# Spacing the steps of four scan cores among the projections of a fused two-block kernel

## The chip, the cores and the metric

The kernel runs on one core of one Trainium2 chip. The metric is the device time of one execution in microseconds (us), the median over runs, so lower is better. Five engines work side by side: TensorE (PE in the profile, its weight loads as PEld), VectorE (DVE), ScalarE (ACT), GpSimd (POOL) and SyncE (SP), which issues the DMAs.

## The reference

Two transformer blocks follow one another on 512 tokens of width 1024, in float32. The first is a two-layer block of mixed attention, and it is not touched here. The second has two layers and works on 768 tokens, 512 latent and 256 context ones. Its first layer mixes tokens by two chunked recurrences run in both directions: an HGRN2 scan and a stabilised mLSTM scan, with four heads each. The outputs are normed per head, gated and projected. What concerns this change is the HGRN2 scan, for one chunk:

```
b = cumsum(logf); b_mid = b[CHUNK//2 - 1]; b_last = b[-1]
A = mask(einsum(q*exp(b - b_mid), k*exp(b_mid - b)))
o = A @ v + (q*exp(b)) @ S
S_new = S*exp(b_last) + (k*exp(b_last - b)).T @ v
```

The mLSTM scan needs, per head and direction, a running sum of log forget gates, a running maximum and exponentials of their differences. That is the gate chain below. Its queries and keys come from a three-tap convolution and a silu.

## The kernel before

Everything here happens in `mixer_ab`, the first layer's mixer of the second block, from about 1209 us to 1661 us of the span. Activations stand with the 1024 features on the partitions in 8 blocks of 128 and the 768 tokens along the free axis, each value split into a high and a low part (`hh`, `hl`). A **projection** (`proj2`, `mm2`, line 1019) multiplies one 128-column unit of weights with all tokens. It loops over the 8 feature blocks and issues six matmuls for each: three passes (high by high, high by low, low by high) on each of two token segments. After each feature block `mm2` calls `tick()`, so a projection has eight **turns**.

What is not a projection hangs on those turns. `later(generator, delay)` puts a generator at the end of a list, and each `tick()` advances the first of the list by one step, after its delay in ticks has run out. The order of PE's instructions is fixed by this program order. For DVE, ACT, POOL and SP the framework picks the order when the kernel is built, by program order as the priority, among what its own timing model takes to be ready. Each engine then runs its list in that order and waits for what an instruction needs. PSUM has 8 banks (tag `b`), SBUF work tiles come from 34 slots (`T()`), and raw weights have 3 buffers (`raw`). Weights come in by SP, are rounded by ACT (`whi`, line 306), and their rest (`wlo`, line 307) is made by POOL in this stage.

The order of the stage, with the turns counted from the first one of the second HGRN projection (the very first is done earlier):

- `hgrn_in(h)` (lines 1209 to 1267) for h = 0, 1, 2 issues four projections of head h: two forget gates, queries and values. Behind the second one stands the **preparation** of the head: sigmoids and a log on ACT, and on DVE a scan (L1234), small factor tiles `fa` (L1243 to L1249, 4 buffers, two to a head) and the scaling of keys (L1257). Head 0 ends at turn 24, head 1 at turn 56, head 2 at turn 88. In `hgrn_in(1)` and `hgrn_in(2)` a step of the gate chain is issued behind each of the first three projections, so behind turns 32, 40, 48, 64, 72 and 80.
- `hgrn_core(h)` (lines 1269 to 1368) has 18 steps. Step 1 transposes the values (L1053, copies on ACT L1059). Steps 2 and 3 make the masked scores of the two directions (L1284, L1286) and scale keys (L1289). Steps 4 and 5, one for each direction, make the **small products** of 32 by 32 (L1301), whose copies go out on DVE (L1303), and scale keys on DVE (L1305) and queries on POOL (L1306). Steps 7 and 8 make blocks of 64 (L1316, ACT copy L1318, scalings L1323). Steps 10 and 11 transpose the keys. Steps 12 to 17 are the recurrence over six 128-token blocks: L1343, L1348 and L1350 on PE, state updates L1355 and L1357 on DVE. Step 18 closes with a norm (POOL L1499, DVE L1501 and L1505). Steps 6 and 9 issue nothing. Core 0 waits 24 turns and takes turns 49 to 66, core 1 takes 67 to 84, core 2 89 to 106.
- The **gate chain** (`gate_chain`, lines 1102 to 1175) has six steps. On DVE: step 1 L1105, L1106 and L1109; step 2 L1114 and two scans of L1123; step 3 L1129 and two scans of L1123; step 4 L1136 to L1146; step 5 L1150 and L1155; step 6 two of L1161. Step 4 stores `cm` by SP (L1147) and step 5 stores `wi` (L1153). A last call queues `by_token`, six and six transposes that the mLSTM heads need.
- Four convolutions `conv(j)` (lines 1181 to 1202, turns 89 to 120): a projection each, then L1191, L1195, L1196, L1197 on DVE and silu on ACT.
- `hgrn_in(3)` (turns 121 to 152). Core 3 follows with a delay of 2 (turns 155 to 172).
- Four value projections (`values`, to turn 184), each followed by `later(mlstm_head(h), 2)`, and eight gate projections (`gate`, to turn 248). The mLSTM heads take turns 175 to 226, and `finish(0)` to `finish(3)` (transposes L1512, DVE L1514) turns 227 to 238.
- After turn 248, `drain()` issues whatever is left in the list with no projection in between. Then come `finish(4)` to `finish(7)`, and `place(h)` for all heads (ACT L339, DVE L340), which writes the operand of the next projection (`out2`, L1607). That one takes features 0 to 6 first and 7 last.

The few lines that fix the order of the stage, and the inner loop of a small-product step:

```
for h in range(3):
    self.later(hgrn_core(h, *hgrn_in(h)), 24 if h == 0 else 0)
for _ in chain:
    pass
for j in range(4):
    conv(j)
self.later(hgrn_core(3, *hgrn_in(3)), 2)
```

```
for i in range(2):
    ko, qo = 64 * i + 32 * d, 64 * i + 32 * (1 - d)
    for t in range(n):
        nc.tensor.matmul(pv[ko:ko + 32, t, qo:qo + 32], ...)
    nc.vector.tensor_copy(am[d][ko:ko + 32, a:a + n, qo:qo + 32], pv[ko:ko + 32, 0:n, qo:qo + 32])
```

Of the kernel before, what the change touches and what calls it, by code (L numbers as in the profile page):

```python
# [259 lines left out]
class Body:  # L260
# [763 lines left out]
    def T(self, dt=F32):  # L1024
        return self.ar.tile([P, self.width], dt, tag="t", bufs=self.nslots, name=self.nm("t"))
# [35 lines left out]
    def mixer_ab(self, r):  # L1061
# [114 lines left out]
        chain = gate_chain()  # L1176
# [4 lines left out]
        def conv(j):  # L1181

            ps = self.proj2(self.SEG, "bqk", j)
            z = T()
            b = self.small(2)
            nc.vector.tensor_copy(b, ps[:, 0, SC:SC + 2])
            nc.vector.memset(z[:, 0:1], 0.0)
            nc.vector.memset(z[:, SC + 1:SC + 2], 0.0)
            nc.vector.memset(z[:, T2 + 2:T2 + 3], 0.0)
            for o, w, bk, s in ((1, SC, 0, 1), (SC + 2, S, 1, 0)):  # L1190
                nc.vector.tensor_tensor(z[:, o:o + w], ps[:, bk, 0:w], r[:, o - 1 - bk:o - 1 - bk + w], ALU.mult)  # L1191
                nc.scalar.activation(z[:, o:o + w], z[:, o:o + w], AF.Identity, bias=b[:, s:s + 1])
            cv = T()
            n = T2 + 1
            nc.vector.tensor_scalar(cv[:, :n], z[:, 1:n + 1], c2("conv", 4 + j), None, ALU.mult)  # L1195
            nc.vector.scalar_tensor_tensor(cv[:, :n], z[:, 0:n], c2("conv", j), cv[:, :n], ALU.mult, ALU.add)  # L1196
            nc.vector.scalar_tensor_tensor(cv[:, :n], z[:, 2:n + 2], c2("conv", 8 + j), cv[:, :n], ALU.mult, ALU.add)  # L1197
            o = T()
            self.act(o[:, 0:SC], cv[:, 0:SC], AF.Silu)
            self.act(o[:, SC:T2], cv[:, SC + 1:n], AF.Silu)  # L1200
            qk.append(o)
# [7 lines left out]
        def hgrn_in(h):  # L1209
            z, zb = [], []  # L1210
            for d in range(2):
                t = T()
                zb.append(self.scaled(t, self.proj2(self.SEG, ("hg", h), d), r))
                z.append(t)
                if h:
                    next(chain, None)
            sg, sn = [], []
            for d in range(2):
                nb = self.small(2)
                nc.vector.tensor_scalar(nb, zb[d], -1.0, None, ALU.mult)  # L1220
                x, y = z[d], T()
                self.both(lambda c, s: self.act(y[:, c], z[d][:, c], AF.Sigmoid, bias=nb[:, s:s + 1], scale=-1.0))
                self.both(lambda c, s: self.act(x[:, c], z[d][:, c], AF.Sigmoid, bias=zb[d][:, s:s + 1]))
                sg.append(x)
                sn.append(y)
            self.log_exp()
            res = []
            for d in range(2):
                f = sg[d][:, :T2]
                nc.vector.tensor_scalar(f, f, omlb[:, d, h:h + 1], lbd[:, d, h:h + 1], ALU.mult, ALU.add)  # L1230
                nc.scalar.activation(f, f, AF.Ln)
                bb = T()[:, :T2]
                sd = (1, -1)[d]
                nc.vector.tensor_tensor_scan(bb[:, ::sd], m32, f[:, ::sd], 0.0, ALU.mult, ALU.add)  # L1234
                mid, last = ((15, 31), (16, 0))[d]
                fi, se = (0, 1)[::(1, -1)[d]]
                b3, b4 = ch(bb, 32), bb.rearrange("p (m i n) -> p m i n", i=2, n=32)

                fa = self.ar.tile([P, 66], F32, tag="fa", bufs=4, name=self.nm("fa"))
                lm = self.ar.tile([P, 12, 2], F32, tag="lm", bufs=2, name=self.nm("lm"))  # L1240
                f1, gk, hv, dec = fa[:, 0:12], fa[:, 12:24], fa[:, 48:60], fa[:, 60:66]
                qh = fa[:, 24:48].rearrange("p (m i) -> p m i", i=2)
                nc.vector.tensor_tensor(lm, b4[:, :, :, last], b4[:, :, :, mid], ALU.subtract)  # L1243
                nc.vector.tensor_tensor(f1, lm[:, :, fi], b4[:, :, se, mid], ALU.add)
                nc.vector.tensor_copy(gk, lm[:, :, se])
                nc.vector.tensor_copy(qh[:, :, fi], b4[:, :, fi, mid])
                nc.vector.tensor_tensor(qh[:, :, se], b4[:, :, se, mid], b4[:, :, fi, last], ALU.add)
                nc.vector.tensor_tensor(hv, b4[:, :, 0, last], b4[:, :, 1, last], ALU.add)
                nc.vector.tensor_tensor(dec, hv[:, ::2], hv[:, 1::2], ALU.add)  # L1249
                nc.scalar.activation(fa, fa, AF.Exp)  # L1250
                bm = f
                nc.vector.tensor_tensor(ch(bm, 32), b3, b3[:, :, mid:mid + 1].to_broadcast([P, 24, 32]), ALU.subtract)
                e1 = bb
                nc.scalar.activation(e1, bm, AF.Exp)
                nc.scalar.activation(bm, bm, AF.Exp, scale=-1.0)
                kk = sn[d][:, :T2]
                nc.vector.scalar_tensor_tensor(kk, kk, omlb[:, d, h:h + 1], bm, ALU.mult, ALU.mult)  # L1257
                res.append([e1, kk, None, fa])
            q = T()
            self.addb(q, self.scaled(q, self.proj2(self.SEG, ("hg", h), 2), r))  # L1260
            if h:
                next(chain, None)
            for d in range(2):
                nc.gpsimd.tensor_tensor(res[d][0], res[d][0], q[:, :T2], ALU.mult)
            vf = T()
            self.addb(vf, self.scaled(vf, self.proj2(self.SEG, ("hg", h), 3), r))
            return vf, res

        def hgrn_core(h, vf, res):
# [4 lines left out]
            for d in range(2):  # L1274
                q, k, _, fa = res[d]
# [15 lines left out]
            for d in range(2):  # L1291
                q, k, _, fa = res[d]

                for a, n in ((0, 2), (2, 4)):
                    ps = self.aux()
                    pv = ps.rearrange("p (t e) -> p t e", e=P)
# [3 lines that stand above are left out]
                            o = (a + t) * P  # L1300
                            nc.tensor.matmul(pv[ko:ko + 32, t, qo:qo + 32], k[:, o + ko:o + ko + 32], q[:, o + qo:o + qo + 32],  # L1301
                                             start=(t == 0), stop=(t == n - 1), skip_group_check=True)
                        nc.vector.tensor_copy(am[d][ko:ko + 32, a:a + n, qo:qo + 32], pv[ko:ko + 32, 0:n, qo:qo + 32])  # L1303
                kh, qb = k.rearrange("p (m n) -> p m n", n=64), ch(q, 32)
                nc.vector.tensor_tensor(kh, kh, fa[:, 12:24].unsqueeze(2).to_broadcast([P, 12, 64]), ALU.mult)  # L1305
                nc.gpsimd.tensor_tensor(qb, qb, fa[:, 24:48].unsqueeze(2).to_broadcast([P, 24, 32]), ALU.mult)  # L1306
                yield
            yield
            for d in range(2):
                q, k, _, fa = res[d]  # L1310

                ko, qo = 64 * d, 64 * (1 - d)
# [22 lines left out]
            for i in range(6):  # L1335
                for d in range(2):
                    q, _, kt, fa = res[d]
# [179 lines left out]
        def place(h):  # L1517

            for a, n in ((0, 2), (2, 4)):
                hc = (slice(CO, CO + SC), slice(LT, LT + S))[a // 2]  # L1520
                self.split(self.hh[:, h, hc], self.hl[:, h, hc], gates[h][0][:, a * P:(a + n) * P])

        for h in range(3):
            self.later(hgrn_core(h, *hgrn_in(h)), 24 if h == 0 else 0)
        for _ in chain:
            pass
        for j in range(4):
            conv(j)
        self.later(hgrn_core(3, *hgrn_in(3)), 2)
        for h in range(4):  # L1530
            values(h)
            self.later(mlstm_head(h), 2)
# [501 lines left out]
```

## Time and profile before

| what | us |
|---|---|
| median of 3 runs (2975.01 to 2976.49) | 2975.02 |
| the profiled execution | 2982.45 |
| its span, first to last instruction | 2980.2 |
| `mixer_ab` in the span, first to last projection | 1208.7 to 1661 |

PE is busy for 95% of the span, DVE for 63%, ACT for 40% and POOL for 19%. The DMA engines carry 93 GB/s on average. The page has the span in 40 slices of 74.5 us. A digit is a busy share in tenths, and the line PEclk is the clock that TensorE was granted. An entry in the list of waits reads as "engine, tile and line that waited <- what released it: us in total, times, the longest". In a timeline a row is start, duration, engine, line and operation, with "[idle before <-releaser]" where the engine stood still ahead of it. Durations on POOL are rough, and ends of matmuls are modelled, so starts are the safer number.

### The profile page before, as it was taken

To read this page: it belongs to the slowest core of one execution; us is meant where nothing else is said; L and a number is where in the kernel's file an instruction comes from. 1 tells how busy PE (TensorE), PEld (TensorE's weight loads), DVE (VectorE), ACT (ScalarE), POOL (GpSimd) and SP (SyncE) were. 2 spreads that over 40 slices of the span, in tenths; PEclk is the share of its full clock that TensorE was granted. 3 is DMA by queue.
4 is the path that set the end of the run, shared out by engine and by line. 5 is a ranking of instruction groups with operands and counts; after the bars stand their busy time and mean duration, and the time that the engine had idled before them with its cause. 6 is when DMAs were issued, how large, how long until landed. Compare 5 with 4: busy or idle time off the path is not lost. (4 is left out here: it accounts for less than half of the span.)

```text
span 2980.2 us, 42310 instructions
## 1 busy us (share of the span) xinstructions
PE 2845.4 (95%) x16554; PEld 2479.1 (83%) x16554; DVE 1874.6 (63%) x3532; ACT 1192.8 (40%) x2085; POOL 560.6 (19%) x437
## 2 busy tenths in 40 slices
PE   9999999999999999978999999999999899999997
PEld 7777888877778888867777988888888888899997
DVE  7679995477689985766544373343335788544445
ACT  5663222346542223523444453122113577532223
POOL 3630000036310001533332140000001420300002
PEclk9999999999999999989999999999999999999998
DMA  4235663331156652210121302221121210233332
GB/s 144 74 99 177 199 195 105 92 111 60 64 184 200 195 166 92 82 34 29 43 88 40 107 29 71 64 64 59 62 64 57 86 43 13 91 96 94 98 92 71
DMA packets 98935, 278.46 MB, mean 93 GB/s; under 512 B 11504, under 2 KB 16880, under 8 KB 98224
## 3 DMA queue, kind: packets, MB, share of 16 engines
q1 hardware_dynamic: 98736, 275.76, 29.4%
q8 instruction: 130, 2.13, 0.3%
q14 instruction: 69, 0.57, 0.1%
HBM read 264.84 MB, written 6.68 MB: 91 GB/s over the span
## 5 line engine op out<-in xcount | busy, mean ns | idle before, releaser
L306 ACT ACTIVATE whi<-raw 128x1024 fp32r<-128x1024 f32 (+1 forms) x363 | 377.9, 1042 | 1218.9 <-PE b L1019 451.3
L1019 PE MATMUL b<-hh,whi 128*128 128x512 f32 (+1 forms) x2000 | 649.3, 325 | 0.0
L1019 PE MATMUL b<-hh,wlo 128*128 128x258 f32 x2000 | 476.2, 320 | 0.0
L1019 PE MATMUL b<-hl,whi 128*128 128x512 f32 (+1 forms) x2000 | 470.5, 317 | 0.0
L307 DVE TENSOR_TENSOR wlo<-raw,whi 128x1024 fp32r<-128x1024 f32 (+1 forms) x321 | 391.7, 1220 | 102.4 <-ACT whi L306 100.6
L1019 PEld LDWEIGHTS b<-hh,whi 128*128 128x128 f32 x2000 | 379.9, 190 | 33.5 <-issue 4.0
L1019 PEld LDWEIGHTS b<-hl,whi 128*128 128x128 f32 x2000 | 349.4, 189 | 50.5 <-issue 0.2
L1019 PEld LDWEIGHTS b<-hh,wlo 128*128 128x128 f32 x2000 | 314.5, 191 | 0.0
L334 PE MATMUL b<-hbl,whi 128*128 128x512 f32 x704 | 275.2, 391 | 2.6 <-DVE hbl L345 2.6
L869 DVE SCALAR_TENSOR_TENSOR junk<-araw,cond 128x512 f32<-128x512 f32 x384 | 271.8, 708 | 8.5 <-ACT cond L355 2.3
L333 PE MATMUL b<-hbh,whi 128*128 128x512 f32 x704 | 275.8, 392 | 1.0 <-ACT hbh L344 1.0
L335 PE MATMUL b<-hbh,wlo 128*128 128x512 f32 x704 | 275.1, 391 | 0.3 <-DVE wlo L307 0.3
L1592 POOL TENSOR_TENSOR acc<-acc,t 128x256 f32<-128x256 f32 (+1 forms) x54 | 48.9, 906 | 1015.0 <-ACT t L1587 1014.1
L1019 PE MATMUL b<-t,whi 128*128 128x512 f32 (+1 forms) x864 | 212.5, 354 | 0.0
L392 POOL TENSOR_TENSOR acc<-acc,sq 128x512 f32<-128x512 f32 (+1 forms) x33 | 47.4, 1437 | 761.9 <-ACT sq L389 761.3
L1019 PEld LDWEIGHTS b<-t,whi 128*128 128x128 f32 x864 | 162.3, 188 | 29.7
L334 PEld LDWEIGHTS b<-hbl,whi 128*128 128x128 f32 x704 | 132.8, 189 | 31.4 <-DVE hbl L345 3.3
L333 PEld LDWEIGHTS b<-hbh,whi 128*128 128x128 f32 x704 | 132.7, 189 | 29.2 <-ACT hbh L344 1.5
L335 PEld LDWEIGHTS b<-hbh,wlo 128*128 128x128 f32 x704 | 132.8, 189 | 28.8 <-DVE wlo L307 1.0
L307 POOL TENSOR_TENSOR wlo<-raw,whi 128x1024 fp32r<-128x1024 f32 x42 | 107.4, 2559 | 188.3 <-ACT whi L306 182.8
L335 PE MATMUL b<-hidh,wlo 128*128 128x512 f32 (+1 forms) x352 | 134.2, 381 | 1.2 <-DVE wlo L307 1.1
L333 PE MATMUL b<-hidh,whi 128*128 128x512 f32 (+1 forms) x352 | 133.8, 380 | 0.0
(452 smaller groups left out, 5754.0 us busy)
## 6 DMA issues: line engine op xcount, KB each, us to landing
raw<-w SPq DMA_DIRECT2D x365, 512.0 KB, 3.5
araw<-ada SPq DMA_DIRECT2D x192, 256.0 KB, 3.0
raw<-w SPq DMA_DIRECT2D x18, 256.0 KB, 2.7
xr<-xd SPq DMA_DIRECT2D x2, 2048.0 KB, 8.2
t<-dm SPq DMA_DIRECT2D x8, 384.0 KB, 5.2
x<-xT SPq DMA_DIRECT2D x8, 256.0 KB, 5.3
kTh<-krh SPq DMA_DIRECT2D x32, 64.0 KB, 2.0
kTl<-krl SPq DMA_DIRECT2D x32, 64.0 KB, 2.0
```

Source lines behind the costliest of these rows:

```text
L306: self.last = nc.scalar.activation(hi[:, :m], r, AF.Copy).ins
L307: self.lo_eng.tensor_tensor(lo[:, :m], r, hi[:, :m].bitcast(F32), ALU.subtract)
L333: t.matmul(out, ah, bh, start=start, stop=False, skip_group_check=True)
L334: t.matmul(out, ah, bl, start=False, stop=False, skip_group_check=True)
L335: t.matmul(out, al, bh, start=False, stop=stop, skip_group_check=True)
L392: nc.gpsimd.tensor_tensor(acc[:, c], acc[:, c], t[:, c], ALU.add)
L869: nc.vector.scalar_tensor_tensor(junk, raw, 1.0, self.cond[:, s, k], ALU.mult, ALU.mult, accum_out=self.adah[:, i, t, s:s + 1])
L1019: t.matmul(ps[:, b, :w_], w[:, s], x[:, o:o + w_], start=(k == 0 and b not in seen), stop=(k == n - 1 and i == 2), skip_group_check=True)
L1592: nc.gpsimd.tensor_tensor(ac, ac, t, ALU.add)
```

## The change

Three edits, all in `mixer_ab`. The generators of the HGRN cores are wrapped so that after each step one turn passes in which nothing of the list is issued. The small products of a bank are issued for both quadrants before the copies. The calls of the gate chain move: one stays in `hgrn_in(1)`, behind the query projection and the preparation, and the others stand before and after the convolutions.

```
@@ in hgrn_in(h)
                 z.append(t)
-                if h:
-                    next(chain, None)
...
             self.addb(q, self.scaled(q, self.proj2(self.SEG, ("hg", h), 2), r))
-            if h:
+            if h == 1:
                 next(chain, None)
@@ in hgrn_core
                             nc.tensor.matmul(pv[ko:ko + 32, t, qo:qo + 32], k[:, o + ko:o + ko + 32], q[:, o + qo:o + qo + 32],
                                              start=(t == 0), stop=(t == n - 1), skip_group_check=True)
+                    for i in range(2):
+                        ko, qo = 64 * i + 32 * d, 64 * i + 32 * (1 - d)
                         nc.vector.tensor_copy(am[d][ko:ko + 32, a:a + n, qo:qo + 32], pv[ko:ko + 32, 0:n, qo:qo + 32])
@@ at the end of mixer_ab
+        def spaced(gen):
+
+            for _ in gen:
+                yield
+                yield
+
         for h in range(3):
-            self.later(hgrn_core(h, *hgrn_in(h)), 24 if h == 0 else 0)
+            self.later(spaced(hgrn_core(h, *hgrn_in(h))), 24 if h == 0 else 0)
+        for j in range(4):
+            next(chain, None)
+            conv(j)
+            next(chain, None)
         for _ in chain:
             pass
-        for j in range(4):
-            conv(j)
-        self.later(hgrn_core(3, *hgrn_in(3)), 2)
+        self.later(spaced(hgrn_core(3, *hgrn_in(3))), 2)
```

## Rows read from the trace of the kernel before

**Rows 1.** The page, parts 1 and 2: busy time of the engines, PE by slice.
```profile
PE 2845.4 (95%) x16554; PEld 2479.1 (83%) x16554; DVE 1874.6 (63%) x3532; ACT 1192.8 (40%) x2085; POOL 560.6 (19%) x437
...
PE   9999999999999999978999999999999899999997
```

**Rows 2.** Busy time by stretch: the four HGRN cores, first transposes to last recurrence step.
```profile
core 0: us, PE busy (x) PEld busy (x) DVE busy (x) ACT busy (x) POOL busy (x), PEclk, DMA share, GB/s
1261.20:1313.16 51.96, 37.31 (x276) 32.79 (x274) 34.37 (x70) 13.52 (x23) 16.83 (x9) 0.80 0.09 25
1315.35:1364.56 49.21, 37.66 (x275) 32.64 (x274) 35.05 (x64) 20.95 (x35) 16.71 (x9) 0.93 0.12 37
1371.86:1411.58 39.72, 35.39 (x274) 31.09 (x275) 21.01 (x46) 11.06 (x19) 10.42 (x7) 0.96 0.10 27
1469.75:1507.56 37.81, 34.91 (x274) 30.83 (x275) 17.79 (x36) 9.16 (x16) 11.43 (x9) 0.95 0.19 57
```

**Rows 3.** Waits of PE from 1205 to 1664 us, the longest six.
```profile
PE b L1301 <- DVE t L1303: 15.8, 16, 5.0
PE b L1301 <- DVE fa L1244: 6.6, 1, 6.6
PE b L1348 <- ACT t L1059: 5.7, 2, 4.3
PE b L1053 <- ACT t L1045: 4.7, 4, 3.3
PE b L1455 <- issue: 3.6, 1, 3.6
PE b L1350 <- DVE hR L1357: 3.3, 2, 1.8
```

**Rows 4.** Timeline of PE, 1653 to 1656 us: the first matmul of two turns.
```profile
1653.06 0.40 PE L1019 MATMUL b<-hh,whi 128*128 128x512 f32 x1
...
1654.12 0.40 PE L1019 MATMUL b<-hh,whi 128*128 128x512 f32 x1
```

**Rows 5.** Waits of PE from 1466 to 1508 us, core 3.
```profile
PE b L1301 <- DVE t L1303: 2.5, 4, 1.3
```

**Rows 6.** Busy time in the 14 us in which core 0 stood still longest (columns as above).
```profile
1261.00:1275.00 14.00, 7.24 (x55) 6.40 (x53) 13.94 (x26) 4.84 (x9) 5.01 (x2) 0.90 0.13 37
```

**Rows 7.** Groups of DVE instructions from 1205 to 1664 us: busy us in all, mean ns.
```profile
L1123 DVE TENSOR_TENSOR_SCAN t<-t,t 32x768 f32<-32x768 f32 x4 | 9.2, 2301 | 0.0
...
L1195 DVE TENSOR_SCALAR t<-t,vec 128x769 f32<-128x769 f32 x4 | 7.9, 1977 | 3.4 <-ACT t L1192 3.4
...
L1514 DVE SCALAR_TENSOR_TENSOR t<-b,vec,t 128x256 f32<-128x256 f32 (+1 forms) x11 | 6.5, 603 | 6.2 <-PE b L1512 6.1
...
L1196 DVE SCALAR_TENSOR_TENSOR t<-t,vec,t 128x769 f32<-128x769 f32 x4 | 4.1, 1022 | 0.1
...
L1191 DVE TENSOR_TENSOR t<-b,acc 128x256 f32<-128x256 f32 (+1 forms) x8 | 4.1, 549 | 0.0
...
L1150 DVE TENSOR_TENSOR t<-so,t 64x768 f32<-64x768 f32 x1 | 2.6, 2605 | 0.0
...
L1155 DVE TENSOR_TENSOR t<-t,t 64x768 f32<-64x768 f32 x1 | 0.9, 942 | 0.0
```

**Rows 8.** Timeline of DVE, 1660 to 1671 us, at the end of the stage.
```profile
1660.49 0.42 DVE L1033 TENSOR_TENSOR t<-b,acc 128x256 f32<-128x256 f32 x1 [2.16 <-PE b L1019]
...
1664.15 2.85 DVE L1514 SCALAR_TENSOR_TENSOR t<-b,vec,t 128x512 f32<-128x512 f32 x5
1666.91 3.83 DVE L340 TENSOR_TENSOR hl<-t,hh 128x256 fp32r<-128x256 f32 x8
```

**Rows 9.** Waits of SP's queue from 1205 to 1664 us: the second store of the chain.
```profile
SPq L1153 <- ACT t L1152: 19.9, 1, 19.9
```

**Rows 10.** Timelines of POOL and of DVE around 1264 us.
```profile
1261.96 3.85 POOL L307 TENSOR_TENSOR wlo<-raw,whi 128x1024 fp32r<-128x1024 f32 x1 [6.85 <-ACT whi L306]
...
1264.53 2.10 DVE L1129 TENSOR_TENSOR t<-t,t 64x768 f32<-64x768 f32 x1
```

## The prediction

> **What bounds the kernel now.** I read the page first. PE is busy for 95% of the span and its slices are full nearly everywhere, with a dent at slices 18 and 19 (1267 to 1416 us), which lie in this stage [rows 1]. So a gain must come from time in which PE stands still or runs at its lower clock, and the stage holds some. Next I cut the stage into the four stretches of the HGRN cores [rows 2]. Each holds the same 16 turns and the same small matmuls, so the four lengths should agree. They are 51.96, 49.21, 39.72 and 37.81 us. The list of PE's waits says what it stood for: 15.8 us for the copies of the small products, 6.6 for the factors `fa`, 5.7 for transposed keys or values, 4.7 for the values of a head, 3.3 for state updates [rows 3]. Where core 0 stood longest, DVE was busy for 13.94 of 14 us [rows 6]. It had the preparation of head 1, two steps of the gate chain and core 0 at once. Over the whole span DVE has room (63%). Its work is only bunched.
>
> **What an undisturbed core would take.** A turn takes 1.06 us [rows 4], so 16 turns take 17.0. The best core took 37.81. Of the 20.8 left, 2.5 are waits for the copies [rows 5]. The granted clock was 0.95 there, which is full speed (2.4 GHz) with a piece at 1.2 GHz, and costs about 0.05 x 37.8 = 1.9. So the small matmuls take about 16.4, and an undisturbed stretch 33.4. The four cores lose 18.6, 15.8, 6.3 and 4.4, together 45.1 us. Before cores 2 and 3 PE also waited for the values of the head, which is most of the 4.7 of [rows 3] (longest 3.3). I take 4.0, so 49 us are within reach.
>
> **Edit 1, the spacing.** Counted out by the program, core 0 now takes turns 49 to 83, core 1 84 to 118, core 2 119 to 153, `by_token` 154, core 3 158 to 192, the mLSTM heads 195 to 246, and `finish(0)` 247 and 248. The projections end at turn 248 as before. No instruction is added. Between two steps there are now two turns, 2.1 us instead of 1.06, in which a copy, a scaling or a state update can land. The cores meet other company:
> - Core 0 meets the end of head 1's preparation, without the chain steps that stood in [rows 6]. Its recurrence (turns 71 to 81) falls beside head 2's preparation, as core 1's does now. That company now costs 4.3 (longest wait for transposed keys) and 3.3 [rows 3]. With twice the gap I take half, 4.
> - Core 1 runs wholly beside the convolutions and the chain. I price this under edit 3.
> - Core 2's recurrence (turns 141 to 151) falls beside head 3's preparation, without chain or convolutions: 3.
> - Core 3 starts 3 turns (3.2 us) later than now, about as long as PE waited for its values (3.3), and then has little beside it: 1.
>
> Core 0's `fa` is in use until turn 79, while head 2 asks for one at turn 72, and there are four. So head 2's factors come later. Core 2 wants them at turn 123, 44 turns on, and that covers it. Tiles live longer. I count at most 30 of the 34 slots in use, so no wait there. If that cover were gone, a projection's evacuation would wait for a core's tile, a turn or two each time.
>
> **Edit 1, the end.** Of four `finish` only the first has a projection over it. Numbers 1 to 3 (18 transposes, 6 DVE instructions) fall into the drain, and `place(0)` to `place(3)` are pushed behind them. Now the last gate is ready at 1660.49 and the last `place` ends at 1670.74, after 10.2 us [rows 8], with DVE as the limit. Afterwards DVE has 14 instead of 8 of L1514 at 0.60 us [rows 7] and 16 instead of 8 of L340 at 3.83/8 = 0.48 [rows 8], which is 3.6 + 3.8 = 7.4 us more, plus one operation of the last norm over 768 elements, 0.9 as for L1155 [rows 7]. The 18 transposes are issued after turn 248 rather than before, so the gates end sooner, by 18 x 0.09 = 1.7 us (a stretch has 274 matmuls [rows 2], 96 of them the turns', and the other 178 take 16.4). Net cost 6.6 us. The next projection takes features 0 to 6 first, but its matmuls come faster (under 1 us a feature) than DVE delivers, so PE waits for nearly all of it. Bounds: 3, if half of the places still fit beforehand, and 12, if the norm of the last mLSTM head lands late and PE restarts at 1.2 GHz.
>
> **Edit 2, copies last.** PE no longer waits inside a bank. That removes 2.5 per undisturbed core [rows 5] and the 8 that head 0 takes of the 15.8 (15.8 less three times 2.6) [rows 3]. All of it is inside the 49. The copies, then the scalings behind them, come no later than now. If DVE is late, the wait goes to the next step that reads the scaled keys, four turns on.
>
> **Edit 3, the chain.** Nothing is added here either. Step 1 stays near head 1, steps 2 to 6 go around convolutions 0 and 1. On DVE they need 9.2 for four scans, 2.6 for L1150 [rows 7], 2.1 for L1129 [rows 10], and L1114, L1146, L1155 and two of L1161 at the 0.94 of L1155, so 4.7. Eight tiny ones in step 4 make about 1 (my estimate). Sum 19.6. A convolution needs 1.98 + 2 x 1.02 + 2 x 0.55 = 5.1 [rows 7]. The stretch of turns 89 to 120 takes 48 us on PE: 32 x 1.06 = 34 and about 14 of core 1's 16.4, as its first three steps are over. DVE has in it the chain 19.6, three convolutions 15.3 (the fourth falls behind), core 1 about 15 (17.79 in core 3's stretch, with two evacuations [rows 2]), and a norm with one evacuation, 3.5. That is 53 us into 48. DVE falls about 5 us behind there, and I take 8 for core 1 with some clock lost. Waits behind this: the chain's two stores now stand in SP's queue among these weight loads. The second held SP for 19.9 us before [rows 9] and delayed no projection, as raw weights are three deep. A projection with four spaced steps takes about 12 us, so two of them cover it. If DVE's lag added over 10 us to that wait, each further microsecond would be PE's. Silu and exponentials alternate once more on ACT, at a 40% load, hidden.
>
> **The Trainium skill against edit 3.** A subtraction on POOL took 3.85 us while DVE was in L1129, and L1129 took 2.10 [rows 10], where L1155, of the same size, took 0.94 and L1150 took 2.6 [rows 7]. The chain's seven two-input operations thus cost between 0.94 and 2.6 each. "SBUF — State Buffer", section "Who interferes with whom", says that a DVE instruction with two SBUF inputs contends with a GpSimd instruction that reads SBUF, and that whoever comes first blocks the other. The trace agrees in the durations just given. By that rule, the chain moved beside core 1's POOL scalings would pay the blocked price throughout, which is the second rival below. The sum above goes by the durations measured.
>
> **Sum.** 49 - (4 + 8 + 3 + 1) - 6.6 = 26.4 us off the profiled execution of 2982.45, so 2956.05. That execution stands 7.43 above the median of the runs shown, and I carry this over: 2948.6. The 3.6 us wait of an mLSTM head [rows 3] and the slow matmuls behind it belong to steps that are not spaced. I leave them, with +-8 for the new company.
>
> **Rivals.**
> 1. *Forecast.* 2948.6, own range 2930 to 2962. Chance 0.66.
> 2. *DVE becomes the bound in the convolutions.* For: 53 into 48 us, and [rows 6] shows what a full DVE does. The chain's seven two-input operations at 2.6 each make 18.2 instead of the 9.4 in my sum (4.7 + 2.6 + 2.1), 8.8 more. With the lag in each of three convolutions core 1 loses 22 instead of 8. Against: each step has twice the gap. 2948.6 + 14 = 2962.6. Chance 0.17.
> 3. *Slower: DVE serves preparations, convolutions and chain ahead of the cores' small updates.* Program order is the priority, and a step's copy is issued behind the whole preparation or convolution that went before. Recurrences of cores 0 and 2 would lose the 8.6 that core 1 loses now plus as much again in clock (17 each), and core 1 some 7 us at each of three boundaries, 21: together 55, more than the 49 recovered. With 6.6 at the end the time is 2975 + 13 = 2988. It decides once a spaced step waits about 1 us on average (42 us over 42 steps that issue DVE work). Against: core 2 beside two convolutions lost 6.3 in all. Chance 0.08.
> 4. *The spacing doesn't do what it says.* What PE gains in the cores is given back where the mLSTM heads are pushed against the gates and the drain: 2975. For: they end 20 turns later. Against: they get as many turns as before and the drain issues only 18 transposes. Chance 0.09.
>
> **Numbers.** What a measurement of this kernel can tell from no change is about 0.2%, 6 us. Case 1 lies below 2969 wholly, case 2 for nine tenths (0.15 of its 0.17); its rest and case 4 are the same. Faster 0.81, same 0.11, slower 0.08. The range: residual waits of 5 and an end of 3 give 2975 - 41 = 2934, and the mLSTM wait could take 4 more off. Residual waits of 30 and an end of 12 give 2975 - 7 = 2968. So 2930 to 2970, which takes in case 2 and leaves out cases 3 and 4.
>
> **What would show it.** Right: the four stretches of 32 turns between first transposes and last recurrence step come to 51 to 59 us each (2 x 17.0 + 16.4 = 50.4 undisturbed, plus my residues), with a granted clock near 1; waits of L1301 for L1303 vanish; the last `place` ends about 17 us after the last gate; DVE is at nine tenths during the convolutions. Wrong: DVE full for over 50 us with PE waiting for L1357 or L1059 there; a long wait of L1019 for weights behind a store; or a stretch from last gate to next projection's seventh feature well over 20 us.

## The result, and the profile after

The changed kernel takes 2940.1 us (median of four runs, 2938.5 to 2943.9) against 2975.8 us for the kernel before (four runs beside it, 2975.0 to 2977.4). The ratio is 0.988, with an interval of 0.9868 to 0.9892: faster by 1.2%, and 8.5 us below the forecast of 2948.6. The profiled execution took 2943.85 us with a span of 2941.8.

The page of the changed kernel, parts 1 and 2, the answer to [rows 1]:

```profile
PE 2824.8 (96%) x16554; PEld 2463.4 (84%) x16554; DVE 1864.7 (63%) x3532; ACT 1197.9 (41%) x2090; POOL 562.6 (19%) x437
...
PE   8999999999999999999999989999999999999997
```

The dent at slices 18 and 19 is gone and the counts of PE and DVE instructions are the same. The next view is the busy time by stretch of the four cores, first transposes to last recurrence step, columns as in [rows 2]:

```profile
1260.04:1320.16 60.12, 52.82 (x372) 46.44 (x370) 43.76 (x92) 26.45 (x42) 24.40 (x11) 0.94 0.13 36
1323.42:1377.73 54.31, 50.98 (x371) 45.27 (x370) 47.50 (x79) 23.48 (x35) 23.87 (x15) 0.97 0.18 54
1380.99:1434.75 53.76, 49.98 (x371) 44.19 (x370) 32.75 (x74) 24.50 (x40) 21.23 (x11) 1.00 0.14 40
1443.59:1492.71 49.12, 49.12 (x371) 43.88 (x370) 19.02 (x41) 12.62 (x21) 14.91 (x11) 1.00 0.23 73
```

Each stretch now holds 32 turns instead of 16, hence some 371 matmuls instead of 275, so the lengths aren't to be set against those before as they stand. Core 3 is the yardstick: PE is busy for all of its 49.12 us at a clock of 1.00. Take 32 turns at 1.06 off, and the small matmuls of a core take 15.2 us by this; with 1.066 for a turn (the five from 1208.85 us on, which hold nothing else, take 5.33) it is 15.0. The waits of PE in this stage, the answer to [rows 3]:

```profile
PE b L1299 <- DVE fa L1247: 3.8, 1, 3.8
PE b L1512 <- DVE t L1505: 3.7, 1, 3.7
PE b L1343 <- DVE t L1191: 3.0, 1, 3.0
PE b L1455 <- issue: 2.6, 2, 2.0
PE b L1348 <- ACT t L1059: 2.6, 1, 2.6
PE b L1350 <- DVE hR L1357: 2.0, 2, 1.5
```

The waits of the small products for their copies, 15.8 us before, are not in this list any more (L1299 is the product's new line, L1301 was its old one). What is left on top is one wait of 3.8 us of core 0's small products, one of 3.0 in core 1, and a new one of 3.7 us at the end, at L1512, which transposes the normed outputs of a head.

Two of the names in this list need care. DVE's instructions count up one semaphore, and the list names the one that ended last before PE went on, which need not be the one that PE needed. The small products read keys and queries and no factor tile. The 3.8 us end when L1287 has scaled the keys of core 0; PE and DVE there:

```profile
1273.63 0.69 PE L1299 MATMUL b<-t,t 128*32 128x32 f32 x24 [3.78 <-DVE fa L1247]
```

```profile
1272.94 0.54 DVE L1287 TENSOR_TENSOR t<-t,fa 128x384 f32<-128x384 f32 x1
1273.40 0.15 DVE L1247 TENSOR_TENSOR fa<-fa 128x6 f32<-128x6 f32 x1
```

The tile that L1247 writes belongs to head 1. The 6.6 us that [rows 3] puts down to L1244 is the same wait: there too the scaling of the keys (L1289) ends 0.15 us before PE starts. So the prediction named the wrong tile for it; that DVE was late with head 1's preparation in front is right. L1343 reads nothing of L1191 either. L1191 empties the bank of a convolution, so this wait is, as I read it, for a free PSUM bank.

**Where the time came from.** The stage, from its first projection to the first matmul of the next stage's projection, took 454.3 us before (1208.8 to 1663.1) and takes 423.5 (1207.6 to 1631.1): 30.9 less. The two as one row each, before and after:

```profile
1208.75:1663.06 454.31, 412.97 (x2602) 348.28 (x2601) 261.76 (x541) 192.24 (x358) 158.14 (x91) 0.95 0.16 49
```

```profile
1207.60:1631.06 423.46, 401.00 (x2602) 340.08 (x2601) 253.13 (x541) 200.28 (x367) 159.54 (x91) 0.98 0.18 54
```

PE stands still for 41.3 us before and 22.5 after (length less busy time), 18.9 less. The same 2602 matmuls keep it busy for 12.0 us less, at a granted clock of 0.98 instead of 0.95. So almost two fifths of the gain is clock.

The spans differ by 38.4. Of the rest 1.2 lies ahead of the stage and 6.4 behind it, in code that the change doesn't touch. The largest piece there, 3.9, is a stretch of later projections; 20 us of it in each kernel, before and then after, from the same instruction on:

```profile
2330.00:2350.00 20.00, 16.06 (x102) 15.16 (x102) 15.83 (x24) 8.61 (x21) 11.01 (x13) 0.84 0.29 106
```

```profile
2297.00:2317.00 20.00, 17.22 (x124) 16.23 (x122) 16.51 (x27) 10.12 (x23) 9.98 (x12) 0.96 0.34 117
```

The same work ran at a granted clock of 0.84 in one and 0.96 in the other. Over the twelve runs below, all of which leave it untouched, the part behind the stage took 1310.6 to 1319.1 us. So up to 8 us between two executions are not the stage's own, and I read parts of the stage from traces and totals from medians. The changed kernel's two profiled executions agree in this part (1310.7 each); whether the stage's end has an effect on it is not shown.

### The profile page after: what moved, and what is told of

Read it like the earlier page. It is cut to its first block, busy times and chain, and to the rows that moved or that the text cites. A ratio compares the mean times of both kernels' runs of the same rounds, so it can differ in the third digit from the quotient of the medians.

```text
span 2941.8 us, 42299 instructions
## 1 busy us (share of the span) xinstructions
PE 2824.8 (96%) x16554; PEld 2463.4 (84%) x16554; DVE 1864.7 (63%) x3532; ACT 1197.9 (41%) x2090; POOL 562.6 (19%) x437
## 5 line engine op out<-in xcount | busy, mean ns | idle before, releaser
L307 DVE TENSOR_TENSOR wlo<-raw,whi 128x1024 fp32r<-128x1024 f32 (+1 forms) x321 | 391.4, 1220 | 97.9 <-ACT whi L306 96.2
L333 PEld LDWEIGHTS b<-hbh,whi 128*128 128x128 f32 x704 | 132.7, 189 | 29.4 <-ACT hbh L344 1.5
L307 POOL TENSOR_TENSOR wlo<-raw,whi 128x1024 fp32r<-128x1024 f32 x42 | 106.3, 2532 | 171.4 <-ACT whi L306 140.3
L1663 DVE COPY sml<-b 128x2 f32<-128x2 f32 x44 | 7.0, 160 | 200.8 <-PE b L1019 200.8
```

What stands on the lines that cost most here:

```text
L307: self.lo_eng.tensor_tensor(lo[:, :m], r, hi[:, :m].bitcast(F32), ALU.subtract)
L333: t.matmul(out, ah, bh, start=start, stop=False, skip_group_check=True)
L1663: nc.vector.tensor_copy(bu, pu[:, 0, bcol])
```

## The experiments

Twelve runs, five rounds each, against the kernel before beside them (2975.8 to 2976.9 us). The changed kernel, run again at the end:

> The changed kernel itself once more, as the measure on this chip for the other three: 2938 to 2942.

It took 2940.5 us, ratio 0.9881 (0.9867 to 0.9894).

### Which edit brings how much

**Without the spacing** (edits 2 and 3 stay):

```diff
-            self.later(spaced(hgrn_core(h, *hgrn_in(h))), 24 if h == 0 else 0)
+            self.later(hgrn_core(h, *hgrn_in(h)), 24 if h == 0 else 0)
...
-        self.later(spaced(hgrn_core(3, *hgrn_in(3))), 2)
+        self.later(hgrn_core(3, *hgrn_in(3)), 2)
```

> The changed kernel with edit 1 undone: cores step at every turn again, copies stay last, the chain stays around the convolutions. Theory (the time came mostly from the spacing): waits of PE for state updates, transposed keys and scaled keys come back in the cores, while the end of the stage is short again (place within about 10 us of the last gate). 2940 + 24 - 7 = about 2957. Rival (the time came from taking the chain away from the cores of heads 0 and 1 and from the copies; spacing only adds an open end): 2935 or less.

Measured: 2950.6 us, 0.9909 (0.9895 to 0.9924). It lies between the two expectations and nearer to the theory's. In this company the spacing is worth about 10 us net. The profiled execution is the slowest of this kernel (2958.1), and it shows more than the theory's waits. Up to the first L1455, PE stands still for 21.6 us here and for 14.4 in the changed kernel. The end is shorter by 9.3 us, as forecast. But the first mLSTM head, 20 turns earlier than in the changed kernel, waits 3.6 us at L1455 instead of 2.0, and behind that stands

```profile
1500.00:1520.00 20.00, 20.00 (x65) 14.06 (x64) 4.62 (x22) 4.47 (x15) 0.00 (x0) 0.52 0.01 1
```

A granted clock of 0.52 over 20 us costs about 9.6. So in this execution a good part of what the spacing brings stands in the mLSTM head and not in the cores; how much of it stands in the other executions is not shown.

**Only the spacing** (the kernel before with edit 1):

> The kernel before with edit 1 alone. Theory: waits between steps go, waits for copies inside a step stay at about 16 us, and the end is open (12 us from last gate to next projection): 2962 to 2966, like the changed kernel without edit 2, as the chain's place decides nothing. Rival (the chain beside the preparations and the copies together fill DVE, and spacing alone doesn't help): 2972 or more.

Measured: 2962.0 us, 0.9945 (0.9933 to 0.9958), as the theory had it. The trace shows what the spacing alone does not do. PE's waits in this stage:

```profile
PE b L1301 <- DVE t L1303: 14.9, 16, 4.8
```

Two turns between steps leave the copies' waits where they were, 14.9 us against 15.8 [rows 3]. They stand inside a step.

**Without the copies' move** (edits 1 and 3 stay):

```diff
-                    for i in range(2):
-                        ko, qo = 64 * i + 32 * d, 64 * i + 32 * (1 - d)
                         nc.vector.tensor_copy(am[d][ko:ko + 32, a:a + n, qo:qo + 32], pv[ko:ko + 32, 0:n, qo:qo + 32])
```

> The changed kernel with edit 2 undone: a copy follows each quadrant's products again. Theory: the wait stands inside one step, so spacing can't cover it. PE waits for L1303 again, 2.5 to 3.4 us a head, 10 to 14 in all: about 2952. Rival (with one more turn between steps DVE is so early that the copies cost nothing): 2940 to 2942.

Measured: 2963.3 us, 0.9957 (0.9946 to 0.9969): 23 us above the changed kernel, more than either expected. PE's waits in the stage:

```profile
PE b L1299 <- DVE t L1301: 16.3, 16, 5.2
```

The waits explain 16 of them. The matmuls also run slower: over three equal stretches of 60 us the granted clock is 0.91, 0.89 and 0.94, and in the changed kernel over the same stretches 0.94, 0.97 and 1.00. The second stretch in the kernel without the move, and in the changed one:

```profile
1320.00:1380.00 60.00, 49.65 (x323) 43.10 (x324) 49.91 (x86) 23.15 (x38) 22.67 (x15) 0.89 0.13 39
```

```profile
1320.00:1380.00 60.00, 56.67 (x405) 50.26 (x404) 50.91 (x82) 28.81 (x45) 27.06 (x16) 0.97 0.17 51
```

In the same 60 us PE gets 82 more matmuls through, while DVE is as busy. From its first scores (L1282) to its last recurrence matmul the four cores take 63.8, 60.0, 56.2 and 49.3 us here, and 57.6, 51.8, 51.2 and 46.6 in the changed kernel. The differences add up to 22.1, nearly the 23 us measured.

**Only the copies' move** (the kernel before with edit 2):

> The kernel before with edit 2 alone: both quadrants' products ahead of the copies. Theory (a wait inside a step can't be covered from outside, and costs its length plus matmuls at 1.2 GHz behind it): the waits for the copies go in all four heads, 16 us of waits and 3 to 6 us of clock: 2955 to 2958. Rival (without spacing the same wait only moves to the next step that needs DVE): 2966 or more.

Measured: 2959.6 us, 0.9936 (0.9924 to 0.9949), about the theory's. Alone the two lines are worth 17 us. The waits for the copies go, the other large ones of [rows 3] stay, and one grows:

```profile
PE b L1301 <- DVE fa L1244: 6.6, 1, 6.6
PE b L1350 <- ACT t L1059: 5.4, 2, 3.9
PE b L1053 <- ACT t L1045: 4.7, 4, 3.3
PE b L1352 <- DVE hR L1359: 4.4, 1, 4.4
```

The last is a state update, 4.4 us where [rows 3] has 3.3 in all: with the products no longer held up, the next step comes sooner and, as I read it, waits there. With the spacing it is 2.0, and the 4.7 for the values of a head is gone.

**Without the chain's move** (edits 1 and 2 stay; the chain's steps go back into the preparations of heads 1 and 2):

```diff
                 z.append(t)
+                if h:
+                    next(chain, None)
...
-            if h == 1:
+            if h:
                 next(chain, None)
...
         for j in range(4):
-            next(chain, None)
             conv(j)
-            next(chain, None)
```

> The changed kernel with edit 3 undone: the chain's steps stand in the projections of heads 1 and 2 again. Theory: core 0 meets the chain beside the preparations and loses some 10 us more, core 1 beside the convolutions alone loses 5 less: 2945. Rival (DVE is the bound in the convolutions, so the chain is better off where it was): 2933 or less.

Measured: 2939.6 us, 0.9881 (0.9868 to 0.9894), the same as the changed kernel. Both expectations were wrong: with spaced cores the chain's place makes no difference that can be measured. Without the spacing it does: edits 2 and 3 together took 2950.6 and edit 2 alone 2959.6, and their intervals only touch (the one ends at 0.9924, the other begins there). Edit 3 by itself was not tried. In the traces the waits change places: with the chain where it was, core 0 waits 4.9 us at its first small products and core 1 2.1, and in the changed kernel 3.8, and 3.0 for the bank.

So the copies alone bring 17 us, the spacing alone 15, and both together 37 (the run without the chain's move, 2939.6 against 2976.6). The third edit adds nothing to these two.

### The open end

The changed kernel pays at the end of the stage. PE's timeline there, start and duration first:

```profile
1619.22 3.80 PE L1512 MATMUL b<-cst,t 128*128 128x128 f32 x30
...
1629.90 1.51 PE L1512 MATMUL b<-cst,t 128*128 128x128 f32 x6 [3.73 <-DVE t L1505]
1631.06 0.78 PE L1615 MATMUL b<-hh,whi 128*128 128x256 f32 x2
```

And DVE's over the same time, the answer to [rows 8]:

```profile
1619.19 0.42 DVE L1033 TENSOR_TENSOR t<-b,acc 128x256 f32<-128x256 f32 x1 [0.34 <-PE b L1019]
...
1624.32 3.63 DVE L1514 SCALAR_TENSOR_TENSOR t<-b,vec,t 128x256 f32<-128x256 f32 x7
...
1628.80 0.95 DVE L1505 TENSOR_TENSOR t<-t,sml 128x768 f32<-128x768 f32 x1
...
1636.78 1.95 DVE L340 TENSOR_TENSOR hl<-t,hh 128x256 fp32r<-128x256 f32 x4
```

After the last gate PE has nothing but transposes until DVE has finished the norm of the last mLSTM head (L1505), which stood in DVE's queue behind nine products of the finishes (L1514), a weight rest (L307) and two of the places (from 1622.05 us on). From the last projection's matmul to the next projection's first it is 2.9 us before and 12.2 after. The last `place` ends at 1638.7, 19.5 us after the last gate.

**The price of the end by itself.** In the kernel before, the first `finish` was delayed by 20 turns, so that all later ones fall into the drain:

```diff
-            self.later(finish(h), 0)
+            self.later(finish(h), 20 if h == 0 else 0)
```

> The kernel before with one edit: finish(0) has a delay of 20 turns, so it stands under the last gate projection and finishes 1 to 3 fall into the drain, as in the changed kernel. Nothing else moves. Theory (the open end costs what DVE needs for six more of L1514 and the places pushed behind them): the next projection starts about 9 us later after the last gate, 6 to 8 us on the whole: 2983 to 2985. Rival (the changed kernel's long end comes from the late norm of the last mLSTM head, which is early here): 2977 to 2979.

Measured: 2979.5 us against 2975.8, 1.0009 (1.0000 to 1.0018): 3.7 us, between the two. In the trace the way from the stage's first projection to the next norm's matmuls takes 510.5 instead of 505.3. So the late finishes cost 4 to 5, and the rest of the changed kernel's end is the norm that lands late: with the `finish` delayed, but the mLSTM heads where they were, PE starts the next projection 7.3 us after the last gate and not 12.2.

**Pulling the end forward.** The delays ahead of core 3 and of the mLSTM heads go from 2 to 0:

```diff
-        self.later(spaced(hgrn_core(3, *hgrn_in(3))), 2)
+        self.later(spaced(hgrn_core(3, *hgrn_in(3))), 0)
...
-            self.later(mlstm_head(h), 2)
+            self.later(mlstm_head(h), 0)
```

> The changed kernel with the delays of core 3 and of the four mLSTM heads at 0 instead of 2, which brings all four finishes (turns 237 to 247) back under the gate projections. Theory (the open end costs 6 to 8 us, as DVE has the late finishes and places in a row): next projection starts about 4 us after the last gate instead of 12, and the time is 2933 to 2935, less 1 or 2 us of new waits in the mLSTM heads. Rival (the open end costs nothing, as PE would have waited for the places anyway): 2940, with the wait moved to the next projection.

Measured: 2952.9 us (2943.3 to 2959.7), 0.9919 (0.9902 to 0.9935). Both missed: it is 13 us slower than the changed kernel. The end did shrink to 4.3 us. But the first mLSTM head now waits longer at L1455. PE's waits, and then the engines by 10 us around that wait:

```profile
PE b L1455 <- issue: 3.8, 1, 3.8
```

```profile
1495.00:1505.00 10.00, 6.17 (x36) 4.97 (x35) 6.86 (x10) 9.94 (x22) 7.41 (x4) 0.84 0.17 58
1505.00:1515.00 10.00, 10.00 (x31) 6.84 (x31) 1.66 (x9) 3.29 (x12) 0.00 (x0) 0.50 0.00 1
1515.00:1525.00 10.00, 10.00 (x32) 7.18 (x32) 3.03 (x13) 2.13 (x6) 0.00 (x0) 0.50 0.00 0
1525.00:1535.00 10.00, 10.00 (x57) 7.76 (x57) 4.18 (x14) 5.94 (x12) 5.99 (x5) 0.97 0.37 133
```

Read the second and third rows. PE is busy for all of the 20 us, nothing is waited for, and yet only 31 and 32 matmuls pass, where the row below has 57: the granted clock is 0.50, the lower level of 1.2 GHz. So behind a wait of 3.8 us stand about 11 us more, lost to the clock, 10 of them in the two rows. It is not the only such place in this trace: around a wait of 0.93 us at L1458 (1571.2) the granted clock is 0.67 and 0.65 in the two stretches of 10 us from 1570 on.

**That wait removed.** L1455 multiplies by the mLSTM head's decay weights. `weights(h)` reads them back from where the gate chain stored them, subtracts on POOL and takes exponentials on ACT. It is now called earlier:

```diff
         for h in range(4):
             values(h)
+            if h == 1:
+                ahead[0] = weights(0)
             self.later(mlstm_head(h), 2)
```

Once with the changed kernel's delays of 2:

> The changed kernel with nothing but the first mLSTM head's weights made after the second value projection. Theory: the 2.6 us wait of the first mLSTM head and the short stretch at 1.2 GHz behind it go, the open end stays: 2935 to 2938. Rival (that wait is for keys, values or scores, not for the weights): 2940.

Measured: 2940.1 us, 0.9874 (0.9859 to 0.9889): no difference from the changed kernel. That is the rival's number, but not its reason: the wait did hang on these weights, as 0.6 us are left of 2.6. The stage is 6.1 us shorter in the profiled execution (417.4), and the part behind the stage is longer by 5.2, so little is left of it in the whole. Whether the second follows from the first stays open.

And once with the delays at 0:

> The kernel with delays 0 for core 3 and the mLSTM heads, and the first mLSTM head's weights made after the second value projection instead of in its own first step. Theory (the kernel with delays 0 lost its gain to one wait of 3.8 us in the first mLSTM head and 22 us at 1.2 GHz behind it): that wait and the low clock are gone, the end is closed: 2927 to 2932, with little spread. Rival (mLSTM heads without a delay wait elsewhere): 2940 or more.

Measured: 2938.0 us (2936.6 to 2943.2), 0.9868 (0.9855 to 0.9882). It missed the theory too. The first wait is gone and the end is short (4.3 us), but the wait at L1458 in a later head stays, 0.94 us, with the low clock behind it; the timeline, and the 10 us behind it:

```profile
1555.47 0.49 PE L1458 MATMUL b<-mC,t 64*128 64x129 f32 x2 [0.94 <-DVE mC L1465]
```

```profile
1560.00:1570.00 10.00, 10.00 (x32) 6.75 (x31) 2.98 (x15) 2.27 (x11) 0.00 (x0) 0.50 0.00 1
```

### A version that beats both

Core 3 had little beside it before the change either, and once begun it lost only its copies' waits [rows 5], which edit 2 removes. So its spacing should bring nothing, and costs the open end. Left dense, with the earlier weights:

```diff
-        self.later(spaced(hgrn_core(3, *hgrn_in(3))), 2)
+        self.later(hgrn_core(3, *hgrn_in(3)), 2)
         for h in range(4):
             values(h)
+            if h == 1:
+                ahead[0] = weights(0)
```

> The changed kernel with core 3 stepping at every turn (its DVE company is light), which closes the end, and the first mLSTM head's weights made after the second value projection; the delays of 2 stay. Theory: core 3 loses 1 to 2 us, the end gains 8: 2932 to 2935. Rival (what the end gains is lost to new waits and a low clock in the mLSTM heads, as with delays 0): 2938 to 2941.

Measured: 2931.8 us (2928.4 to 2934.2), 0.9848 (0.9834 to 0.9861), as the theory had it, and 8.7 us below the changed kernel beside it (2940.5). From 1430 to 1620 us, core 3 and all mLSTM heads, PE's longest waits are

```profile
PE b L1617 <- DVE hl L340: 1.0, 1, 1.0
PE b L1455 <- ACT t L1480: 0.3, 1, 0.3
```

and after the last gate PE starts the next projection within 2.9 us, as before the change. The stage takes 410.4 us in this profile. Two things were changed at once here. The earlier weights alone brought nothing that can be measured (above), and a dense core 3 alone was not tried. Up to the first L1455 this kernel takes 278.9 us, and the one without any spacing, where core 3 is dense too, 290.1: that is what spacing the other three brings there.

**The same with the chain in its old place:**

> The same with the chain's steps back in the projections of heads 1 and 2. Theory (with spacing the chain's place decides little, and DVE is less full in the convolutions): 2929 to 2935, at most 5 us below the same kernel with the chain around the convolutions. Rival (the chain's place matters, as it did without spacing): 2940 or more.

Measured: 2932.1 us, 0.9851 (0.9838 to 0.9865): the same once more. The chain's place makes no measurable difference here either.

## Why the prediction was right, point by point

**What an undisturbed core takes.** I had 16.4 us for the small matmuls, read from the best core before by taking waits and clock away. Core 3 after the change shows about 15.0. So the cores lost more than I thought: 37.81 less 17.0 and 15.0 is 5.8 for core 3, and 20.0, 17.2, 7.7 and 5.8 for the four, 50.7 instead of 45.1. The term was too small by 5.6.

**Residues.** Against 49.12 the spaced cores lose 11.0, 5.2, 4.6 and 0. I had 4, 8, 3 and 1. The sum is 20.8 instead of 16, which takes back nearly all of the 5.6: with the 4.0 of values, 33.9 us are recovered, and I had 33. That the two errors cancel is luck. The step that was most mis-sized is core 0's. I had taken the 6.6 us of [rows 3] for a wait for factors, where it was one for scaled keys behind them. I had also written that core 0's company no longer has the chain steps of [rows 6], and halved the waits of core 1. But other chain operations took their place. In [rows 6] stand L1129 and two scans, 5.6 us. In the changed kernel step 1 stands behind head 1's preparation, as I had written under edit 3, and DVE runs L1114 of step 2 there too: L1105, L1106, L1109 and L1114 take 6.4 us of the 20 below. Busy time in the changed kernel, columns as above:

```profile
1260.00:1280.00 20.00, 16.22 (x134) 14.06 (x133) 19.93 (x37) 8.78 (x14) 12.85 (x5) 0.91 0.10 27
```

DVE has no gap in 20 us, and core 0's first small products wait 3.8 us for the scaled keys. Four rows of DVE's timeline in this stretch:

```profile
1262.77 2.02 DVE L1105 TENSOR_SCALAR t<-t,sml 64x256 f32<-64x256 f32 x1
...
1268.82 0.18 DVE L1242 TENSOR_TENSOR fa<-lm,t 128x12 f32<-128x12 f32 x1
...
1270.52 1.80 DVE L1242 TENSOR_TENSOR fa<-lm,t 128x12 f32<-128x12 f32 x1
...
1277.16 2.23 DVE L1114 SCALAR_TENSOR_TENSOR t<-t,t 64x768 f32<-64x768 f32 x1
```

L1242, the same instruction on twelve columns, takes 0.18 and 1.80 us. The second ran while POOL was in a product of two tiles:

```profile
1270.01 2.28 POOL L1262 TENSOR_TENSOR t<-t,t 128x768 f32<-128x768 f32 x1 [5.36 <-ACT t L1252]
```

Both ended together, at 1272.3. The Trainium skill, "SBUF — State Buffer", section "Who interferes with whom", says that a DVE instruction with two SBUF inputs contends with a GpSimd instruction that reads SBUF, and that the order of issue decides which one is held up. The trace agrees, with 1.80 us against 0.18. Of the 20 us, one instance each of L1105, L1242, L1287 and L1114, all four beside POOL, took 7.9 together; the same four forms take 2.0 together elsewhere in these two traces. I had put this harm into the convolutions (rival 2). A good part of it was at core 0.

**Core 1, the convolutions, and edit 3.** I gave core 1 a residue of 8 from a DVE that is 5 us short. DVE is busy for 47.50 of 54.31 us there, 87%, near the nine tenths forecast, and core 1 loses 5.2, of which 3.0 is the wait for the bank behind L1191. The 53 us in 48 did not come: in turns 89 to 120 DVE is busy for 42.9 of 51.8 us. It is full for the first 30 us only (29.4, with the chain's steps 2 to 4). Most of the chain's operations that I feared did not become dear:

```profile
L1123 DVE TENSOR_TENSOR_SCAN t<-t,t 32x768 f32<-32x768 f32 x4 | 8.9, 2227 | 0.1
...
L1114 DVE SCALAR_TENSOR_TENSOR t<-t,t 64x768 f32<-64x768 f32 x1 | 2.2, 2227 | 0.0
...
L1129 DVE TENSOR_TENSOR t<-t,t 64x768 f32<-64x768 f32 x1 | 0.9, 942 | 0.0
L1150 DVE TENSOR_TENSOR t<-so,t 64x768 f32<-64x768 f32 x1 | 0.9, 942 | 0.0
```

L1150 and L1129 fell from 2.6 and 2.1 [rows 7, 10] to 0.94. Three rose beside POOL: L1114, at head 1's preparation, from 0.95 to 2.2, the first of L1105 from 0.34 to 2.0, and L1136, a scan of six columns, from 0.15 to 2.15. One of L1106 fell, from 1.84 to 0.35. The runs agree: the place of the chain is worth nothing that can be measured with the spacing. I had added no instruction for the edit, but charged core 1 with 8 for it. The two stores that I had watched hold SP for 12.5 and 7.5 us, where the second alone held it for 19.9 [rows 9], and no projection waited.

**Edit 2.** I had 15.5 us for it, inside the 49. Undoing it cost 23 and it brings 17 alone. The waits themselves I had right (15.8 in the trace). What I left out of this term is the clock that falls behind them; in the sum it was counted, since the losses of the cores contain it.

**The end.** I had 6.6 net, with 3 to 12 as bounds. From the last gate to the matmuls of the next norm (L940) it is 53.9 us before and 63.1 after: 9.3, less the 1.7 that the transposes no longer take ahead (my estimate), 7.6. The bound of 12 named the norm of the last mLSTM head landing late, and that is part of what came: a wait of 3.73. The delayed `finish` shows the rest at 4 to 5, less than the 6.6 that I had worked out from DVE's instructions alone.

**What I left out.** The mLSTM heads I carried with nothing and +-8. Before, the 3.6 us wait of L1455 [rows 3] was followed by some 10 us at the lower clock; after, the waits come to 2.6, the longest 2.0, and the clock falls far less. Before, and then after:

```profile
1525.00:1535.00 10.00, 9.88 (x31) 7.09 (x32) 2.15 (x10) 2.61 (x10) 0.00 (x0) 0.51 0.00 0
```

```profile
1510.00:1520.00 10.00, 10.00 (x48) 7.13 (x47) 4.56 (x17) 5.55 (x14) 1.62 (x1) 0.83 0.40 131
```

The stage came out 30.9 shorter. Cores 33.9 less 7.6 for the end make 26.3, the sum I had (26.4), for other reasons in each of two terms. The 4.6 that are left are of the size of this wait and these slow matmuls: 1.0 less waiting, and 4.9 less 1.7 of clock in the two rows. I infer that from the windows; no run isolates it. The rest of the 8.5 us from 2948.6 to 2940.1, about 4, lies outside the stage, which no step of mine was about, or in the 7.43 that I carried over from one execution.

**The rivals.** Rival 2 (DVE the bound in the convolutions) has its mechanism in the 30 us in which DVE is full and in the wait of 3.0, at a fraction of its price. Rival 3 (slower) needed a wait of 1 us at each spaced step; PE stands still for 7.3, 3.3, 3.8 and 0 us in the four stretches (length less busy time), 14.4 instead of 42. Rival 4 (given back in the mLSTM heads and the drain) has its mechanism in the 7.6 us, but not its size. Signs named beforehand: stretches of 51 to 59 us (60.1, 54.3, 53.8 and 49.1, so core 0 and core 3 fall outside by 1 to 2), a granted clock near 1 (0.94 to 1.00), no waits of products for copies (so), last `place` about 17 us after the last gate (19.5).

## What to carry to other kernels

Compare stretches that hold the same work: their best one, cleared of its waits, tells what the others can win, and after the change that yardstick should be read again. Within a step, issue all of a bank's products before its first copy; space steps out only where the neighbour fills the engine that serves them, since every spaced step also moves the end of the queue into a drain that has nothing to hide it. The best version here spaces three of the four cores. And read a gain by stretches: part of it can stand in a neighbour that only starts at another moment, as in the first mLSTM head here.

## What the hardware showed that I had not expected

What a wait of PE costs is not its length. A wait of 3.8 us was followed by 20 us and more at a granted clock of 0.50 although PE was busy throughout, one of 0.94 us by a whole 10 us slice at 0.50, and one of 2.0 us by a slice at 0.83. Behind them stands the same kind of work, small matmuls of mLSTM heads between turns. The kernel with the 3.8 us wait also spread most from run to run (2943 to 2960 us).

Waits as long in the HGRN cores cost less. The 10 us behind the 3.8 us wait of core 0 and behind the 3.0 us wait of core 1, in the kernel that beats both:

```profile
1270.90:1280.90 10.00, 9.60 (x84) 7.88 (x84) 9.91 (x11) 2.37 (x4) 10.00 (x4) 0.83 0.10 18
1355.00:1365.00 10.00, 9.85 (x67) 8.93 (x68) 8.59 (x18) 8.82 (x11) 0.00 (x0) 1.00 0.32 87
```

No run here varies the work behind one and the same wait, so what decides how long the clock stays low is open.
